# Gated-branch values: 512 weight columns per matmul and two k-chunks per load, instead of 256 columns and four k-chunks

## Chip, cores and metric

One Trainium2 core of a chip runs one launch. The metric is device time in microseconds (us); lower is better. Three timed runs of the kernel before gave 1669.36, 1669.82 and 1670.14 us, median 1669.82. All data are float32 in HBM.

## What is computed

One decoder layer over 512 prompt tokens and 64 sample tokens (8 sequences of 8), model width 1024: a SwiGLU feed-forward block, a mixing block, a second feed-forward block, each behind an RMS norm with conditioning. The change lies in the mixing block, in the value half of its gated branch:

```python
z = h @ w_in                      # w_in has 1024 rows; u, v, q, k, rv, rg, ga, gb are column ranges
v = layer_norm(gelu(v), gm_ln_g, gm_ln_b)      # v: 576 tokens x 1024 columns
o_a = gelu(u) * chunk_spatial_mix(v, ...)
o_b = head_rms(retention(rotary(q), rotary(k), rv, state)) * silu(rg)
```

The retention has 8 heads with 128 key and 256 value columns each.

## The kernel before

**Precision.** Large products are made in the float32r format of TensorE. A weight or activation is split into a high part (a cast on ScalarE, L180 in `split_w`, L188 in `split`) and a low remainder (a subtraction on VectorE, L181, L189). A product is the sum of three matmuls: high x high, low x high and high x low. The small products inside a retention head (L1376, L1438, L1454, L1467 to L1482) are plain float32, and the profile records each of these as two passes.

**Where the change sits.** The mixing block runs head by head. For head hd, `values_of` (matmuls L1346 and L1359) makes the head's values; `core(hd)` does the retention itself; `beside(hd)` gives the work that runs on TensorE next to that core. For heads 0 and 1 this work is `values` (matmuls L1576): columns 0 to 511 of v beside head 0 and 512 to 1023 beside head 1. Later heads have output products (`out_b`, L478) or the gates u beside them.

**`values` before.** The 512 columns of a head are done as two halves z of 256 columns. Each half has two loads of 512 KB (`load_w`: four k-chunks of 128 rows by 256 columns, DMA at L169, cast L180, subtraction L181). For each of five token tiles (four of 128 prompt tokens, and the 64 sample tokens, whose high and low parts fill one tile of 128) a PSUM bank is taken, and all 8 k-chunks are accumulated in it: 24 matmuls of 256 columns for a prompt tile, 16 for the sample tile. Then ScalarE takes the gelu out of PSUM at once (L1585; for the sample tile L1587, VectorE L1588 and L1589), and in the second half VectorE makes the statistics (L1591). A head has 224 such matmuls, the two heads 448.

**How the core is mixed in.** `core` is a generator. `tick(us)` (L225) subtracts a written cost from its delay and, when that is used up, issues its next piece. The pieces come at 0.5, 4.5, 8.5, 10.5, 12.5, 14.5, 18.5 and 20.5 us of ticked time. Before, `values` ticks after each token tile: 2.616 us for a prompt tile, 1.744 for the sample tile, 24.4 us in a head. The pieces, by number: 1, scores and transposes (L1376 to L1414), which need the rotated k from GpSimd (L1324); 2, four state products in four banks (L1438), evacuated by VectorE (L1441, L1443); 3, L1454; 4 and 5, the outputs (L1467 to L1482), two banks each; 6, squares and split; 7, two banks of sums over the squares (L1500), which VectorE reads only in piece 8 (L1522), and then four products, each in a bank of its own (L1511), evacuated by VectorE (L1515); 8, the scaling.

**Buffers and order.** PSUM has 8 banks in one pool (`bank`, bufs=8) for everything. Weight loads land in 3 raw buffers, split weights in 4. Banks and buffers are handed out, and the order of instructions on each engine is fixed, when the program is built: a planner goes by the order in which the code issues the work, but it puts an instruction that it takes to be ready ahead of an earlier one that it takes to be waiting. At run time each engine keeps that order.

Of the kernel before, what the change touches and what calls it, by code (L numbers as in the profile page):

```python
# [10 lines left out]
AF = mybir.ActivationFunctionType  # L11
ALU = mybir.AluOpType
# [3 lines left out]
P = 128  # L16
D = 1024
KC = D // P
# [3 lines left out]
NS = NB * LS  # L22
# [59 lines left out]
def layer_kernel(ctx: ExitStack, tc: tile.TileContext, a):  # L82
    nc = tc.nc
    PE, DVE, ACT, POOL = nc.tensor, nc.vector, nc.scalar, nc.gpsimd
# [22 lines left out]
    def nm(s):  # L107
        count[0] += 1
        return f"{s}_{count[0]}"
# [13 lines left out]
    def slot(shape, dt=F32):  # L123

        turn[1] += 1
        if now["slu"] and turn[1] % (NSLOT + NSLOT2) < NSLOT2:
            return now["slu"].tile(shape, dt, tag="c", name=nm("c"), bufs=NSLOT2)
        return now["sl"].tile(shape, dt, tag="c", name=nm("c"), bufs=now["slots"])
# [12 lines left out]
    def bank():  # L141
        return pp.tile([P, 512], F32, tag="ps", name=nm("ps"), bufs=8)
# [24 lines left out]
    def load_raw(src, k0, kc, c0, cols):  # L167
        raw = raw4([kc, cols])
        nc.sync.dma_start(  # L169
            out=raw, in_=src[k0 * P:(k0 + kc) * P, c0:c0 + cols].rearrange("(k p) c -> p k c", p=P)  # L170
        )
        return raw
# [5 lines left out]
    def split_w(raw, eng=None):  # L178
        hi, lo = high_low(list(raw.shape[1:]))
        ACT.copy(out=hi, in_=raw)  # L180
        now["lo"] = (eng or DVE).tensor_tensor(out=lo, in0=raw, in1=hi.bitcast(F32), op=ALU.subtract)  # L181
        return hi, lo

    def load_w(src, k0, kc, c0, cols, eng=None):
        return split_w(load_raw(src, k0, kc, c0, cols), eng)
# [39 lines left out]
    def tick(us):  # L225
        for s in list(side):
            s[1] -= us
            while s in side and s[1] <= 0:
                try:
                    s[1] += next(s[0])  # L230
                except StopIteration:
                    side.remove(s)
# [50 lines left out]
    for i in range(2):  # L283
        for n in range(NT):
            rows = P if n < 4 else NS
            t = first.tile([rows, 512], F32, name=nm("xt"))
# [185 lines left out]
    def proj(w, X, h, kc=KC, c0=0, ks=None, ps=None):  # L472
        ps = bank() if ps is None else ps
        wh, wl = w
        for k in ks or range(kc):
            xh, xl = X[k]
            for z, (s, m) in enumerate(((wh, xh), (wh, xl), (wl, xh))):
                PE.matmul(  # L478
                    ps[:, :H], lhsT=s[:, k, c0:c0 + P], rhs=m[:, HALF[h]],
                    start=k == 0 and z == 0, stop=k == kc - 1 and z == 2,  # L480
                )
        return ps
# [543 lines left out]
    for i in range(2):  # L1026
        for n in range(NT):
            m = P if n < 4 else NS
            ACT.activation(
                out=junk[0:m, i], in_=xtok[n, i], func=AF.Square, accum_out=ss[0:m, i, n:n + 1]  # L1030
# [54 lines left out]
    for c in range(KC):  # L1085
# [5 lines left out]
        out=t5, in0=r5, scalar=-0.5 / D, in1=r5, op0=ALU.mult, op1=ALU.mult)  # L1091
    steps["r51"] = lambda: DVE.scalar_tensor_tensor(
        out=t5, in0=s5, scalar=D * EPS, in1=t5, op0=ALU.add, op1=ALU.mult)
# [3 lines left out]
        out=xall[:, :, NP:T], in_=psS[:, 0:KC * NS].rearrange("p (c t) -> p c t", c=KC))  # L1097
# [22 lines left out]
    win = a["w_in"][0]  # L1120
    U0, V0, Q0, K0, RV0, RG0, GA0, GB0 = 0, 1024, 2048, 3072, 4096, 6144, 8192, 9216
# [158 lines left out]
    rts, tks = [], {}  # L1280
# [251 lines left out]
    def weights_b(hds, j):  # L1532
        kc = 2 * len(hds)
        return load_w(a["w_b"][0], 2 * hds[0], kc, j * (8 // kc) * P, 8 // kc * P)

    def out_b(hds, j, wb, cs=None):

        kc = 2 * len(hds)
        n = 8 // kc
        OB = [x for hd in hds for x in OBs[hd]]  # L1540
        for c in cs or range(n):
            t = slot([P, T])
            for h in range(2):
                ps = proj(wb, OB, h, kc=kc, c0=c * P)
                ACT.copy(out=t[:, HALF[h]], in_=ps[:, :H])
                tick(cost(kc))
            dst = accd[:, n * j + c, :]
            if hds[0] == 0:
                POOL.dma_start(out=dst, in_=t)
            else:  # L1550
                POOL.dma_start(out=dst, in_=t, accum_op=ALU.add)


    v = {}
# [3 lines left out]
    I32 = mybir.dt.int32  # L1558

    def weights_v(i, z):  # L1560
        return [load_w(win, 4 * kk, 4, V0 + i * 512 + z * 256, 256) for kk in range(2)]

    def values(i, z, ws):

        cl = slice(z * 256, (z + 1) * 256)
        for n in range(NT):
            ps = bank()
            for kx in range(KC):
                w = ws[kx // 4]
                if n < 4:  # L1570
                    xh, xl = (x[:, n * P:(n + 1) * P] for x in X[kx])
                    terms = ((xh, w[0]), (xl, w[0]), (xh, w[1]))
                else:
                    terms = ((tks["hs"][:, kx, :], w[0]), (tks["hs"][:, kx, :], w[1]))
                for y, (s, m) in enumerate(terms):
                    PE.matmul(  # L1576
                        ps[:, :256], lhsT=s, rhs=m[:, kx % 4, :], start=kx == 0 and y == 0,
                        stop=kx == KC - 1 and y == len(terms) - 1,
                    )
            m = P if n < 4 else NS  # L1580
            if z == 0:
                v[n, i] = slot([m, 512])
            t = v[n, i][:, cl]
            if n < 4:
                ACT.activation(out=t, in_=ps[:, :256], func=AF.Gelu_apprx_tanh)  # L1585
            else:
                ACT.copy(out=t, in_=ps[NS:P, :256])  # L1587
                DVE.tensor_tensor(out=t, in0=ps[0:NS, :256], in1=t, op=ALU.add)  # L1588
                ACT.activation(out=t, in_=t, func=AF.Gelu_apprx_tanh)  # L1589
            if z:  # L1590
                DVE.bn_stats(out=tks["stats"][0:m, n, i, :], in_=v[n, i])  # L1591
            tick((24 if n < 4 else 16) * 0.109)

    gains = []

# [52 lines left out]
    def weights_u(g):  # L1648
        return load_w(win, 0, KC, U0 + g * P, P)

    def gate_u(g, wu):
        t = slot([P, T])
        for h in range(2):
            ps = proj(wu, X, h)
            ACT.activation(out=t[:, HALF[h]], in_=ps[:, :H], func=AF.Gelu_apprx_tanh)
            tick(cost(KC))
        POOL.dma_start(out=ud[:, g], in_=t)
# [27 lines left out]
    def beside(hd):  # L1685

        if hd < 2:
            for z in range(2):
                yield lambda z=z: weights_v(hd, z), lambda w, z=z: values(hd, z, w)
        elif hd % 2 == 0:  # L1690
            for j in range(4):
                hds = hd - 2, hd - 1
                yield lambda j=j: weights_b(hds, j), lambda w, j=j: out_b(hds, j, w)
        elif hd < HEADS - 1:
            for g in range(2 * hd - 6, 2 * hd - 2):
                yield lambda g=g: weights_u(g), lambda w, g=g: gate_u(g, w)

    for hd in range(HEADS):
        wv = [load_w(win, 4 * i, 4, RV0 + hd * DV, DV) for i in range(2)]
        if hd:  # L1700
            states(hd)
        rv, rvs = values_of(hd, wv, rows[hd][:2])
        OBs.append([])
        q, k, *gates = rows.pop(hd)
        prev = core(hd, q, k, gates, rv, rvs, OBs[hd])
        start(prev, 0.5)
        if hd == 2:
            start(layer_norm(), 4.0)
        work = list(beside(hd))
        ready = None  # L1710
        for i, (weights, f) in enumerate(work):
            f(ready or weights())
            ready = None
            if i == 0 and hd + 1 < HEADS:
                rows[hd + 1] = fetch(hd + 1)
                if hd == 1:
                    fetch_gains()
                if hd == HEADS - 2:
                    fetch_mixers()
            if i == len(work) - 2 and i:  # L1720
                ready = work[i + 1][0]()
        if hd + 1 < HEADS:
            finish(prev)
        if hd == HEADS - 2:
            masks(0)
            masks(1)

    VT = [xx.tile([P, 4, T], F32, tag="x", name=nm("v"), bufs=4) for _ in range(4)]
    for i in range(2):
        for n in range(NT):  # L1730
            m, z = P if n < 4 else NS, NT * i + n
# [89 lines left out]
    for pr in ([0], [1], [2], [3], [4], [5], [6, 7]):  # L1821
# [4 lines left out]
        for h in range(2):  # L1826
            for c in pr:
                ps = proj(W[c], OA, h)
                t = sa[c][:, HALF[h]]
# [218 lines left out]
```

## Time and profile before

| what | value |
|---|---|
| median of the timed runs | 1669.82 us |
| span of the profiled execution, first to last instruction | 1665.5 us |
| median minus that span | 4.3 us |
| TensorE matmul busy | 1636.4 us |
| VectorE, ScalarE, GpSimd busy | 1154.7, 783.7, 287.8 us |
| `values` beside head 0 (with the core's pieces) | 755.62 to 794.16 us |
| `values` beside head 1 | 807.31 to 845.39 us |

The profiled execution gives its span; no other time of its own is recorded, so the 4.3 us around it are taken as they stand to the median. In the rows of the profile PE is TensorE's matmuls, PEld its weight loads, DVE is VectorE, ACT ScalarE, POOL GpSimd and SP the engine that issues loads. A row of the timeline has the start (us from the span's start), the duration, the engine, the line, the operation, output<-input, the shape (stationary rows x columns, then partitions x moving columns), and the count of merged instructions; in brackets stands the idle time of the engine before it and what ended it. Matmuls overlap in the pipeline, so the cost of a run of them is read from its start to the start of the next row, not from its duration.

### The profile page before, as it was taken

To read this page: it belongs to the slowest core of one execution; us is meant where nothing else is said; L and a number is where in the kernel's file an instruction comes from. 1 tells how busy PE (TensorE), PEld (TensorE's weight loads), DVE (VectorE), ACT (ScalarE), POOL (GpSimd) and SP (SyncE) were. 2 spreads that over 40 slices of the span, in tenths; PEclk is the share of its full clock that TensorE was granted. 3 is DMA by queue.
4 is the path that set the end of the run, shared out by engine and by line. 5 is a ranking of instruction groups with operands and counts; after the bars stand their busy time and mean duration, and the time that the engine had idled before them with its cause. 6 is when DMAs were issued, how large, how long until landed. Compare 5 with 4: busy or idle time off the path is not lost. (4 is left out here: it accounts for less than half of the span.)

```text
span 1665.5 us, 31366 instructions
## 1 busy us (share of the span) xinstructions
PE 1636.4 (98%) x12548; PEld 1574.8 (95%) x12548; DVE 1154.7 (69%) x1835; ACT 783.7 (47%) x1331; POOL 287.8 (17%) x372
## 2 busy tenths in 40 slices
PE   7999999999999999999999999999999999999997
PEld 4899999999999999999999999998999999999997
DVE  6867857576797777755688554677748868576773
ACT  5634524344564566544445454443236535243453
POOL 0000000000411110013346343454231000000002
PEclk9999999999999999999999999999999999999999
DMA  9553444332547676764457474799540333332321
GB/s 301 146 156 102 140 136 130 115 102 87 181 127 219 206 223 198 219 202 153 146 180 251 162 179 151 210 263 267 164 140 14 86 92 99 92 90 85 97 86 58
DMA packets 300212, 252.09 MB, mean 151 GB/s; under 512 B 13593, under 2 KB 260633, under 8 KB 300066
## 3 DMA queue, kind: packets, MB, share of 16 engines
q1 hardware_dynamic: 284594, 206.76, 41.2%
q0 software_dynamic: 13168, 40.97, 8.9%
q10 hardware_dynamic: 2304, 2.36, 0.4%
q8 instruction: 98, 1.61, 0.4%
q14 instruction: 48, 0.39, 0.1%
HBM read 207.01 MB, written 43.02 MB: 150 GB/s over the span
## 5 line engine op out<-in xcount | busy, mean ns | idle before, releaser
L644 PE MATMUL ps<-xa,whl 128*128 128x288 f32 x3000 | 421.0, 295 | 4.4 <-ACT whl L662 1.4
L644 PEld LDWEIGHTS ps<-xa,whl 128*128 128x128 f32 x3000 | 402.0, 189 | 17.3 <-issue 4.2
L644 PE MATMUL ps<-xs,whl 128*128 128x288 f32 x2040 | 289.4, 295 | 0.8 <-ACT sn L653 0.4
L644 PEld LDWEIGHTS ps<-xs,whl 128*128 128x128 f32 x2040 | 274.7, 189 | 10.9 <-issue 5.0
L672 DVE TENSOR_TENSOR whl<-wraw,whl 128x1024 fp32r<-128x1024 f32 x192 | 235.0, 1226 | 55.6 <-ACT whl L662 46.0
L662 ACT CAST whl<-wraw 128x1024 fp32r<-128x1024 f32 x192 | 200.3, 1048 | 109.5 <-DVE wraw L786 67.1
L478 PE MATMUL ps<-c,wd 128*128 128x288 f32 x1824 | 246.1, 295 | 0.0
L478 PEld LDWEIGHTS ps<-c,wd 128*128 128x128 f32 x1824 | 242.4, 189 | 3.7 <-issue 3.4
L478 PE MATMUL ps<-c,whl 128*128 128x288 f32 x1368 | 190.5, 297 | 1.1 <-ACT c L188 0.6
L478 PEld LDWEIGHTS ps<-c,whl 128*128 128x128 f32 x1368 | 182.8, 189 | 3.1 <-ACT c L188 1.1
L465 POOL TENSOR_TENSOR x<-x,s 128x64 f32<-128x64 f32 x72 | 34.6, 481 | 808.2 <-DVE s L464 781.0
L459 DVE SCALAR_TENSOR_TENSOR x<-ps,gate,x 128x288 f32<-128x288 f32 (+1 forms) x128 | 61.2, 481 | 117.1 <-PE ps L478 117.0
L181 DVE TENSOR_TENSOR whl<-wraw,whl 128x1024 fp32r<-128x1024 f32 x56 | 78.0, 1394 | 70.2 <-ACT whl L180 69.4
L653 ACT COPY sn<-ps 128x288 f32<-128x288 f32 x195 | 77.1, 398 | 104.2 <-PE ps L644 103.8
L945 ACT CAST wd<-wraw 128x640 fp32r<-128x640 f32 (+2 forms) x58 | 45.4, 783 | 105.6 <-PE ps L478 97.9
L1346 PE MATMUL ps<-whl,xx 128*128 128x256 f32 x768 | 91.5, 280 | 0.0
L1346 PEld LDWEIGHTS ps<-whl,xx 128*128 128x128 f32 x768 | 90.8, 188 | 0.0
L644 PE MATMUL ps<-xs,whs 128*128 128x288 f32 x480 | 69.8, 294 | 0.0
L180 ACT CAST whl<-wraw 128x1024 fp32r<-128x1024 f32 x56 | 58.5, 1049 | 22.7 <-PE ps L478 14.3
L644 PEld LDWEIGHTS ps<-xs,whs 128*128 128x128 f32 x480 | 65.6, 189 | 0.0
L662 ACT CAST whs<-wraw 128x512 fp32r<-128x512 f32 x62 | 38.4, 620 | 57.0 <-PE ps L644 46.7
L950 DVE TENSOR_TENSOR wd<-wraw,wd 128x640 fp32r<-128x640 f32 (+2 forms) x58 | 53.9, 929 | 9.8 <-ACT wd L945 9.8
(285 smaller groups left out, 2222.2 us busy)
## 6 DMA issues: line engine op xcount, KB each, us to landing
ada<-in_w_ada_dram SPq DMA_DIRECT2D x56, 512.0 KB
wraw<-in_w_in_dram SPq DMA_DIRECT2D x96, 256.0 KB
wraw<-in_w_gate_dram SPq DMA_DIRECT2D x88, 256.0 KB
wraw<-in_w_up_dram SPq DMA_DIRECT2D x88, 256.0 KB
wraw<-in_w_in_dram SPq DMA_DIRECT2D x32, 512.0 KB
wraw<-in_w_down_dram SPq DMA_DIRECT2D x32, 384.0 KB
wraw<-in_w_down_dram SPq DMA_DIRECT2D x32, 320.0 KB
accd<-c POOLq DMA_DIRECT2D x32, 288.0 KB, 6.0
```

Source lines behind the costliest of these rows:

```text
L180: ACT.copy(out=hi, in_=raw)
L181: now["lo"] = (eng or DVE).tensor_tensor(out=lo, in0=raw, in1=hi.bitcast(F32), op=ALU.subtract)
L459: DVE.scalar_tensor_tensor(out=x[:, o:o + w], in0=ps[:, :w], scalar=g[:, c, 0:1], in1=x[:, o:o + w], op0=ALU.mult, op1=ALU.add)
L465: return lambda: POOL.tensor_tensor(out=x[:, NP:T], in0=x[:, NP:T], in1=u, op=ALU.add)
L478: PE.matmul(ps[:, :H], lhsT=s[:, k, c0:c0 + P], rhs=m[:, HALF[h]], start=k == 0 and z == 0, stop=k == kc - 1 and z == 2,)
L644: PE.matmul(ps[:, :H], lhsT=s[:, j * P:(j + 1) * P], rhs=m[:, j, :], start=fresh and j == 0 and z == 0, stop=j == 3 and z == 2, skip_group ...
L653: ACT.copy(out=t, in_=ps[:, :H])
L662: ACT.copy(out=hl[:, 0], in_=src)
L672: now["lo"] = DVE.tensor_tensor(out=hl[:, 1], in0=src, in1=hl[:, 0].bitcast(F32), op=ALU.subtract)
L945: ACT.copy(out=hl[:, 0], in_=self.raw[c])
L950: DVE.tensor_tensor(out=lo, in0=self.raw[c], in1=hi.bitcast(F32), op=ALU.subtract)
L1346: PE.matmul(ps[:, :DV], lhsT=s, rhs=m, start=i == 0, stop=i == 23)
```

## The change

The two loads per half become four loads per head, of two k-chunks by 512 columns each; they are still 512 KB each and split by the same number of instructions. The loop over loads is now outermost: for each load, each of the five token tiles gets 6 matmuls of 512 columns (4 for the sample tile), into a bank that is taken at the first load and held until the last. Gelu, the sample tile's sum and the statistics come after the last load, on 512 columns at a time. Ticks come after each tile of each load: 1.32 us (0.88 for the sample tile), 24.64 us in a head. A head has 112 matmuls of 512 columns.

```diff
     def weights_v(i, z):
-        return [load_w(win, 4 * kk, 4, V0 + i * 512 + z * 256, 256) for kk in range(2)]
-
-    def values(i, z, ws):
-
-        cl = slice(z * 256, (z + 1) * 256)
+        return load_w(win, 2 * z, 2, V0 + i * 512, 512)
+
+    vps = {}
+
+    def values(i, z, w):
+
         for n in range(NT):
-            ps = bank()
-            for kx in range(KC):
-                w = ws[kx // 4]
+            if z == 0:
+                vps[n] = bank()
+            ps = vps[n]
+            for kk in range(2):
+                kx = 2 * z + kk
...
                     PE.matmul(
-                        ps[:, :256], lhsT=s, rhs=m[:, kx % 4, :], start=kx == 0 and y == 0,
-                        stop=kx == KC - 1 and y == len(terms) - 1,
+                        ps, lhsT=s, rhs=m[:, kk, :], start=kx == 0 and y == 0,
+                        stop=kx == KC - 1 and y == len(terms) - 1, skip_group_check=True,
                     )
-            m = P if n < 4 else NS
-            if z == 0:
-                v[n, i] = slot([m, 512])
-            t = v[n, i][:, cl]
-            if n < 4:
-                ACT.activation(out=t, in_=ps[:, :256], func=AF.Gelu_apprx_tanh)
-            else:
-                ACT.copy(out=t, in_=ps[NS:P, :256])
-                DVE.tensor_tensor(out=t, in0=ps[0:NS, :256], in1=t, op=ALU.add)
-                ACT.activation(out=t, in_=t, func=AF.Gelu_apprx_tanh)
-            if z:
-                DVE.bn_stats(out=tks["stats"][0:m, n, i, :], in_=v[n, i])
-            tick((24 if n < 4 else 16) * 0.109)
+            if z == 3:
+                m = P if n < 4 else NS
+                t = v[n, i] = slot([m, 512])
+                if n < 4:
+                    ACT.activation(out=t, in_=ps, func=AF.Gelu_apprx_tanh)
+                else:
+                    ACT.copy(out=t, in_=ps[NS:P])
+                    DVE.tensor_tensor(out=t, in0=ps[0:NS], in1=t, op=ALU.add)
+                    ACT.activation(out=t, in_=t, func=AF.Gelu_apprx_tanh)
+                DVE.bn_stats(out=tks["stats"][0:m, n, i, :], in_=t)
+            tick((6 if n < 4 else 4) * 0.22)
...
         if hd < 2:
-            for z in range(2):
+            for z in range(4):
                 yield lambda z=z: weights_v(hd, z), lambda w, z=z: values(hd, z, w)
```

## The prediction, made before the result was known

> **What bounds the kernel now.** I read the page first, then the timeline of the stage that the change touches, then who waited for whom there. The page:
>
> ```profile
> span 1665.5 us, 31366 instructions
> PE 1636.4 (98%) x12548; PEld 1574.8 (95%) x12548; DVE 1154.7 (69%) x1835; ACT 783.7 (47%) x1331; POOL 287.8 (17%) x372
> PE   7999999999999999999999999999999999999997
> PEclk9999999999999999999999999999999999999999
> ```
>
> TensorE's matmuls fill 98% of the span, so a saving must come out of matmul time, and an idle gap that the change puts between matmuls is paid in full. The stage is 742 to 845 us. Its two halves beside heads 0 and 1:
>
> ```profile
> 742.71 11.19 PE L1346 MATMUL ps<-whl,xx 128*128 128x256 f32 x94
> 753.74 2.05 PE L1359 MATMUL ps<-whl,hs 128*128 128x256 f32 x16
> 755.62 2.99 PE L1576 MATMUL ps<-whl,xx 128*128 128x256 f32 x24
> 759.52 1.16 PE L1376 MATMUL ps<-c,c 128*128 128x128 f32 x8 [0.91 <-POOL c L1324]
> ...
> 782.26 5.88 PE L1576 MATMUL ps<-whl,xx 128*128 128x256 f32 x48
> 787.97 0.69 PE L1500 MATMUL ps<-c,onesr 128*128 128x288 f32 x4
> 788.50 1.11 PE L1511 MATMUL ps<-c,c 128*128 128x256 f32 x8
> 789.45 2.98 PE L1576 MATMUL ps<-whl,xx 128*128 128x256 f32 x24
> ...
> 807.31 2.99 PE L1576 MATMUL ps<-whl,xx 128*128 128x256 f32 x24
> 810.14 1.05 PE L1376 MATMUL ps<-c,c 128*128 128x128 f32 x8
> ...
> 838.48 0.44 PE L1500 MATMUL ps<-c,onesr 128*128 128x288 f32 x2
> 838.77 0.39 PE L1511 MATMUL ps<-c,c 128*128 128x256 f32 x2
> 839.60 0.54 PE L1500 MATMUL ps<-c,onesr 128*128 128x288 f32 x2 [0.44 <-DVE c L189]
> 839.97 0.88 PE L1511 MATMUL ps<-c,c 128*128 128x256 f32 x6
> ```
>
> The value matmuls (L1576) and the core's pieces follow each other without a gap, except 0.91 us before L1376 in head 0 (the rotated k was late from GpSimd) and 0.44 before L1500 in head 1. The waits and the use of the engines in the stage:
>
> ```profile
> ACT c L1585 <- PE ps L1576: 26.6, 14, 4.2
> 755.60:794.10 38.50, 37.59 (x330) 36.27 (x329) 21.23 (x31) 18.82 (x33) 13.74 (x15) 1.00 0.39 126
> 807.30:845.40 38.10, 37.66 (x331) 36.34 (x330) 20.94 (x30) 17.42 (x32) 12.42 (x13) 1.00 0.45 146
> ```
>
> The first row says that ScalarE's gelu waits for TensorE, 26.6 us in 14 waits, and not the other way round. The other two are the windows, with the columns PE, PEld, DVE, ACT, POOL, granted clock, DMA share and GB/s: the clock is full, DMA and the other engines have room. So only three things can move the time: the cost of a 512-column matmul, the place of the core's pieces among them, and the banks.
>
> **The change, part by part.** *Matmuls removed and added.* 94 matmuls of 256 columns take 753.74 - 742.71 = 11.03 us, 117.3 ns each; the 448 of `values` go at 448 x 117.3 = 52.6 us. In their place come 224 of 512 columns. No row shows a float32r matmul of that width. The nearest are 288 columns, and a plain-float32 pass of 256 columns:
>
> ```profile
> 525.42 3.31 PE L644 MATMUL ps<-xa,whl 128*128 128x288 f32 x24
> 528.57 3.32 PE L644 MATMUL ps<-xs,whl 128*128 128x288 f32 x24
> 764.38 1.02 PE L1438 MATMUL ps<-c,c 128*128 128x256 f32 x4
> 765.25 0.81 PE L1438 MATMUL ps<-c,c 128*128 128x256 f32 x3
> ```
>
> 288 columns: 3.15 us for 24, 131.25 ns. Upper end: 512 columns cost twice 256, 234.6 ns, and nothing is saved; the cost per column is nearly the same in both rows (0.458 and 0.456 ns), which speaks for it. A line through the two widths (13.95 ns for 32 columns, 0.436 each) gives 117.3 + 256 x 0.436 = 228.9. Lower end: the fifth plain pass starts 0.87 us after the first (the second answer begins with it), 217 ns; a pass that holds the array nearly twice as long as 256 float32r columns do shows only 0.424 ns per column of 512, so part of today's 117.3 may be a fixed cost of a matmul. I take 226, nearer to the line, because its rows are float32r with weight and activation operands: 224 x 226 = 50.6, a saving of 1.9 us; the ends give 4.0 (217) and 0.
>
> The Trainium skill has a rule for this, "TensorE: Matmul & The Clock Gate", section "Back-to-back issue gap": N/2.4 + 2.5 ns when warm, so 109 ns at 256 and 216 at 512 columns. The trace does not agree at 256 (117.3); for a long pass it does (217). By the rule's 512 the saving would be 52.6 - 48.4 = 4.2 us.
>
> *Core pieces.* Six of the eight pieces hold matmuls, before and after, so the number of breaks in the run of value matmuls stays, unless the planner splits more. Piece 1 moves: it came after the first token tile, 24 matmuls; now it comes after the first 6, 6 x 226 = 1.36 us. Head 0's k cannot be there sooner:
>
> ```profile
> 756.01 1.30 DVE L181 TENSOR_TENSOR whl<-wraw,whl 128x1024 fp32r<-128x1024 f32 x1 [1.47 <-ACT whl L180]
> 757.24 0.75 DVE L1323 TENSOR_TENSOR c<-c,rope 128x576 f32<-128x576 f32 x1
> 758.06 1.40 POOL L1324 TENSOR_TENSOR c<-c,c 128x576 f32<-128x576 f32 x1 [1.83 <-DVE c L1323]
> 806.54 1.44 POOL L1324 TENSOR_TENSOR c<-c,c 128x576 f32<-128x576 f32 x1 [0.69 <-DVE c L1323]
> ```
>
> It ends at 759.46, behind a weight split on VectorE that the change leaves there. If L1376 stands right behind the first 6 matmuls, TensorE waits from 756.98 to 759.46, 2.5 us instead of 0.91: +1.6, and behind it on TensorE queue value matmuls that are ready. If the planner sees the wait, it puts the next tile's matmuls first, as it put L1511 between the two L1500 at 838.48: then the wait may shrink below 0.91, at best -0.9. I take +0.5. In head 1 k is there at 807.98, before 807.31 + 1.36 = 808.67: 0; the cover is 0.7 us.
>
> *Banks.* After the first load's tiles five of the eight banks are held, until the last load; three are left for the core. Pieces 3 to 5 take one or two at a time, and ScalarE empties them between. Piece 2 takes four when four are held; the fifth tile's bank then waits for VectorE's first evacuation, and VectorE can be behind by a split (1.30 us above): between 0 and 1.3 a head, mostly covered by the other tiles' matmuls, +0.2 over both. Piece 7 is the tight one. It now comes after the first tile of the last load: two banks for L1500, held until piece 8, and four products that want four more, with one bank free and a second when the first gelu is out. The products are evacuated by
>
> ```profile
> 789.20 2.46 DVE L1515 SCALAR_TENSOR_TENSOR S<-S,ps 128x512 f32<-128x512 f32 x4
> L1511 PE MATMUL ps<-c,c 128*128 128x256 f32 x64 | 9.2, 281 | 0.0
> L1585 ACT ACTIVATE c<-ps 128x256 f32<-128x256 f32 x16 | 6.1, 384 | 26.6 <-PE ps L1576 26.6
> L1487 ACT COPY c<-ps 128x512 f32<-128x512 f32 x16 | 9.4, 587 | 12.9 <-PE ps L1482 12.6
> ```
>
> 0.62 us each. Matmuls of the next tiles (1.36 us a tile, banks already theirs) can stand between the products, so I take 0.3 per head, 0.6 in all; below nothing is excluded, since no wait stands there now. The price without that cover is the second rival.
>
> *The rest, at nothing.* Eight loads stay eight, with the same bytes, casts and splits. On SP three of four loads are now issued after the tiles of the load before, behind the fetch for the next head; with a DMA share of 0.39 and 6.3 us of matmuls per load, a load stays early, and without that cover it would cost its delay. Gelu falls from 16 of 0.384 us to 8 of about 0.6 (the 512-wide L1487 copy takes 0.587) but all at the end of a head, where the next head's first bank is needed one at a time, every 2.8 us (24 matmuls of 117.3): ScalarE's 5 evacuations of about 0.6 us are hidden by that.
>
> **Sum** on the span of 1665.5: -1.9 + 0.5 + 0.2 + 0.6 = -0.6, so 1664.9; with the 4.3 us between span and median, **1669.2 us**. A measurement of this kernel can tell about 0.2%, 3.3 us, from no change: this is none.
>
> **The rivals.**
>
> *The wide matmul is cheap.* If a 512-column matmul costs 217 ns and the fillers hide the waits (k down by 0.4, no bank wait), the sum is -4.0 - 0.4 = -4.4: 1665.4 us, faster. For it: the plain pass at 217. Against it: 0.458 and 0.456 ns per column at 256 and 288, no sign of a fixed part there. Both conditions must hold to pass 3.3 us. The page's rule above stands with this rival.
>
> *Three banks choke piece 7.* If the planner leaves the four products in a row, each waits until VectorE has emptied the one before: latency 0.28 us (the 281 ns of an L1511), 0.24 for its two matmuls (8 in 0.95 us), 0.62 evacuation, 1.14 us. Four take 3 x 1.14 + 0.24 = 3.7 us in place of 0.95: +2.7 a head, +5.4 for two. With k's +1.6 and the saving of 1.9 this gives +5.1: 1674.9 us, slower. It decides when fewer than two spare banks are there at piece 7 and nothing stands between the products. For it: 5 + 2 banks held. Against it: the fill at 838.48 to 839.97, and a gelu that frees a bank within about 1 us.
>
> *Nothing in it.* The width is neutral (234.6 ns) and the small waits come as above: +1.3, 1671.1 us, within 0.2%.
>
> **How the numbers follow.** Forecast 0.47, cheap wide matmul 0.25, choked banks 0.16, nothing in it 0.12. Faster by over 0.2%: 0.25; within 0.2%: 0.59; slower: 0.16. The range runs from 1665.0, just under the cheap case, to 1673.0, which takes in the neutral case with k's full 1.6 us and one bank wait and leaves out most of the choked case. The likeliest case's own range is 1666.5 to 1671.
>
> **What would show it.** In the profile after: value matmuls 128x512, x224; a burst of them read start to start, at 226 ns (217: first rival; 235: third). Between 755 and 795: the idle time before L1376 in head 0, expected 0 to 2.5 us, and whether value matmuls of a second tile stand ahead of it. Before the L1511 rows: no idle time over 0.5 us, and value matmuls between them; a wait for DVE L1515 before each is the second rival. The stage from the first value matmul to the next head's L1346 should go from 38.5 and 38.1 us to about 38 and 37.5. The forecast would be wrong by a wait of several us that I did not place, such as a bank of the next head's L1346 held by a late gelu, or a late weight split of the second load.

## The result and the profile after

The changed kernel takes 1671.14 us (median of 21 runs, 1669.18 to 1674.01) where the kernel before takes 1669.69 on the same chips (21 runs, 1667.57 to 1671.10): a ratio of 1.0012, with a 95% interval of 1.0007 to 1.0018. It is slower by 1.2 to 3.0 us, inside the 0.2% that the prediction called no change; the forecast of a small gain was not met. The profiled execution took 1672.98 us for a span of 1671.2, so 1.8 us lie around the span (the prediction took 4.3, because it compared a quick execution's span with a median).

The page of the changed kernel, its first lines:

```profile
span 1671.2 us, 30923 instructions
PE 1639.1 (98%) x12324; PEld 1567.1 (94%) x12324; DVE 1156.2 (69%) x1833; ACT 782.5 (47%) x1319; POOL 288.2 (17%) x372
```

224 matmuls fewer, as the change says. The share of TensorE's busy time over the whole span tells nothing here; the stage does. The windows run from the first matmul beside a head to the next head's first L1346, beside heads 0, 1 and 2 (columns: length, busy time of PE, PEld, DVE, ACT, POOL, granted clock, DMA share, GB/s). First the changed kernel:

```profile
758.40:796.35 37.95, 37.41 (x219) 30.50 (x218) 20.95 (x28) 16.57 (x25) 13.73 (x15) 1.00 0.44 141
809.50:848.46 38.96, 37.64 (x219) 30.56 (x218) 20.41 (x31) 15.24 (x24) 14.11 (x13) 1.00 0.48 154
861.60:899.90 38.30, 36.90 (x298) 35.22 (x297) 36.36 (x64) 18.16 (x35) 26.50 (x33) 1.00 0.72 237
sum 115.21, PE 111.95 PEld 96.28 DVE 77.73 ACT 49.98 POOL 54.35; mean PE 37.32 PEld 32.09 DVE 25.91 ACT 16.66 POOL 18.12
```

Then the third stretch and the sum of the kernel before (its first two stand in the prediction):

```profile
858.55:895.50 36.95, 36.71 (x298) 35.27 (x297) 34.07 (x58) 18.05 (x35) 26.80 (x32) 1.00 0.71 225
sum 113.55, PE 111.97 PEld 107.89 DVE 76.24 ACT 54.29 POOL 52.96; mean PE 37.32 PEld 35.96 DVE 25.41 ACT 18.10 POOL 17.65
```

This is the result in two rows. TensorE's busy time is the same, 111.95 and 111.97 us, though 224 wide matmuls replaced 448 narrow ones. The stretches are 1.66 us longer, 115.21 against 113.55, and all of that is idle time: 3.26 us after, 1.58 before. Head 0 gains 0.55 us, head 1 loses 0.86, and head 2, whose matmuls the change does not touch, loses 1.35. From head 3 on, the stretches are equal in both kernels (36.51 and 36.46 us, alternating).

Where the idle time lies, by the waits of TensorE between 735 and 900 us in the changed kernel (engine, line, releaser: total, times, longest):

```profile
PE ps L1376 <- POOL c L1324: 3.0, 3, 1.3
PE ps L1414 <- POOL h L1409: 0.3, 1, 0.3
```

The same of the kernel before, and the row of its wait beside head 2 (that of head 0 stands in the prediction):

```profile
PE ps L1376 <- POOL c L1324: 1.1, 2, 0.9
PE ps L1500 <- DVE c L189: 0.4, 1, 0.4
```

```profile
860.54 1.16 PE L1376 MATMUL ps<-c,c 128*128 128x128 f32 x8 [0.24 <-POOL c L1324]
```

And in the timeline of the changed kernel, beside heads 0, 1 and 2:

```profile
758.39 3.39 PE L1579 MATMUL ps<-whl,xx 128*128 128x512 f32 x14
762.32 1.16 PE L1376 MATMUL ps<-c,c 128*128 128x128 f32 x8 [0.54 <-POOL c L1324]
...
789.76 0.70 PE L1500 MATMUL ps<-c,onesr 128*128 128x288 f32 x4
790.29 0.40 PE L1511 MATMUL ps<-c,c 128*128 128x256 f32 x2
790.53 1.33 PE L1579 MATMUL ps<-whl,xx 128*128 128x512 f32 x5
...
793.56 2.02 PE L1579 MATMUL ps<-whl,xx 128*128 128x512 f32 x8
795.42 1.09 PE L1579 MATMUL ps<-whl,hs 128*128 128x512 f32 x4
796.35 0.87 PE L1346 MATMUL ps<-whl,xx 128*128 128x256 f32 x6
...
809.49 1.56 PE L1579 MATMUL ps<-whl,xx 128*128 128x512 f32 x6
812.37 1.16 PE L1376 MATMUL ps<-c,c 128*128 128x128 f32 x8 [1.32 <-POOL c L1324]
...
861.58 1.76 PE L478 MATMUL ps<-c,whl 128*128 128x288 f32 x12
864.47 1.16 PE L1376 MATMUL ps<-c,c 128*128 128x128 f32 x8 [1.13 <-POOL c L1324]
866.74 0.44 PE L1414 MATMUL ps<-ident,h 128*128 128x128 f32 x2 [0.27 <-POOL h L1409]
```

Three things are to be read here. *The width:* the eight matmuls at 793.56 are followed at 795.42, 232.5 ns each; four at 795.42 by 796.35, the same. That is 0.454 ns per column, as at 256 (0.458). *The banks:* pieces 7 and 8 lie at 789.76 to 793.56, value matmuls stand between the L1511, and no row shows a wait. *k:* the L1376 waits for GpSimd's L1324 in all three heads, and in head 1, where there was no wait before, for 1.32 us.

### The profile page after: what moved, and what is told of

The parts are those of the page before. It is cut to its first block, busy times and chain, and to the rows that moved or that the text cites. A ratio compares the mean times of both kernels' runs of the same rounds, so it can differ in the third digit from the quotient of the medians.

```text
span 1671.2 us, 30923 instructions
## 1 busy us (share of the span) xinstructions
PE 1639.1 (98%) x12324; PEld 1567.1 (94%) x12324; DVE 1156.2 (69%) x1833; ACT 782.5 (47%) x1319; POOL 288.2 (17%) x372
## 5 line engine op out<-in xcount | busy, mean ns | idle before, releaser
L644 PE MATMUL ps<-xa,whl 128*128 128x288 f32 x3000 | 425.4, 297 | 4.4 <-ACT whl L662 1.4
L644 PEld LDWEIGHTS ps<-xa,whl 128*128 128x128 f32 x3000 | 406.4, 191 | 17.3 <-issue 4.2
L1346 PE MATMUL ps<-whl,xx 128*128 128x256 f32 x768 | 91.5, 279 | 0.0
L1346 PEld LDWEIGHTS ps<-whl,xx 128*128 128x128 f32 x768 | 90.9, 188 | 0.2
```

Of the source, the lines that this page charges most:

```text
L644: PE.matmul(ps[:, :H], lhsT=s[:, j * P:(j + 1) * P], rhs=m[:, j, :], start=fresh and j == 0 and z == 0, stop=j == 3 and z == 2, skip_group ...
L1346: PE.matmul(ps[:, :DV], lhsT=s, rhs=m, start=i == 0, stop=i == 23)
```

## Why k is late: VectorE at the turn of the heads

VectorE and GpSimd of the changed kernel, from the end of head 0 to k of head 1 (the next value matmul stands at 809.49):

```profile
801.61 1.28 DVE L1592 BATCH_NORM_STATS2 stats<-c 128x6 f32<-128x512 f32 x2
802.81 0.67 DVE L1590 TENSOR_TENSOR c<-ps,c 64x512 f32<-64x512 f32 x1
803.50 0.76 DVE L1320 TENSOR_TENSOR c<-c,rope 64x576 f32<-64x576 f32 x1
...
805.06 0.69 DVE L1592 BATCH_NORM_STATS2 stats<-c 64x6 f32<-64x512 f32 x1
...
806.49 1.99 POOL L1324 TENSOR_TENSOR c<-c,c 128x576 f32<-128x576 f32 x1 [11.02 <-DVE c L1323]
807.20 1.89 DVE L1322 TENSOR_TENSOR c<-c,rope 64x576 f32<-64x576 f32 x1
809.13 0.76 DVE L1323 TENSOR_TENSOR c<-c,rope 128x576 f32<-128x576 f32 x1
809.83 1.22 DVE L181 TENSOR_TENSOR whl<-wraw,whl 128x1024 fp32r<-128x1024 f32 x1
809.97 2.34 POOL L1324 TENSOR_TENSOR c<-c,c 128x576 f32<-128x576 f32 x1 [0.70 <-DVE c L1323]
```

And VectorE of the kernel before (the next value matmul at 807.31; its L1324, 1.44 us at 806.54, stands in the prediction):

```profile
798.83 0.68 DVE L1591 BATCH_NORM_STATS2 stats<-c 64x6 f32<-64x512 f32 x1
799.52 0.75 DVE L1320 TENSOR_TENSOR c<-c,rope 64x576 f32<-64x576 f32 x1
800.29 0.75 DVE L1322 TENSOR_TENSOR c<-c,rope 64x576 f32<-64x576 f32 x1
801.08 1.23 DVE L181 TENSOR_TENSOR whl<-wraw,whl 128x1024 fp32r<-128x1024 f32 x1
```

In the kernel before, gelu and statistics of a tile came every 24 matmuls; one statistic was left at the turn. Now all five tiles of a head end in its last load, so three statistics and the last tile's addition (L1590) queue on VectorE in front of and among the next head's rotary. The rotary of q and k begins 5.99 us ahead of the value matmuls (803.50 against 809.49) in place of 7.79 (799.52 against 807.31): 1.80 later. A split of 1.23 that stood in it is now a statistic of 0.69: 0.54 sooner. GpSimd's last step, now beside a split on VectorE, takes 2.34 in place of 1.44: 0.90 later. Together 2.16; k is there 2.83 us after the first value matmul (809.97 + 2.34 - 809.49 = 2.82), where it was at 0.67 (806.54 + 1.44 - 807.31).

A late k alone would not have cost this in head 1. Before, L1376 stood behind 24 matmuls, 2.83 us; now it stands behind 6 wide ones, 1.4 us.

At the turn from head 1 to head 2 the changed kernel has the same three statistics and the addition, and besides them two steps of the layer norm over v (L1637) in front of the rotary, which in the kernel before come behind its start:

```profile
848.83 0.75 DVE L1637 SCALAR_TENSOR_TENSOR c<-c,mv,c 128x512 f32<-128x512 f32 x1
...
852.63 0.75 DVE L1637 SCALAR_TENSOR_TENSOR c<-c,mv,c 128x512 f32<-128x512 f32 x1
```

## The experiments

What follows is measured by the three stretches of the profiled execution, beside heads 0, 1 and 2, because they came again within 0.05 us in the one repeat made, while the times of one kernel scatter by 3.4 to 7.1 us from run to run (more on this in the last section). The table has them, counted from start to start of the matmuls in the trace. Each ratio is to runs of the kernel before taken beside that kernel, whose own median was between 1669.69 and 1670.17 us:

| kernel | head 0 | head 1 | head 2 | sum | median us (runs) | ratio to before, 95% |
|---|---|---|---|---|---|---|
| before | 38.53 | 38.08 | 36.96 | 113.57 | 1669.69 (21) | |
| after | 37.96 | 38.97 | 38.32 | 115.25 | 1671.14 (21) | 1.0012, 1.0007 to 1.0018 |
| after_again | 37.96 | 39.02 | 38.31 | 115.29 | 1670.93 (1) | |
| e1_halves | 38.59 | 37.47 | 37.80 | 113.86 | 1672.10 (11) | 1.0014, 1.0005 to 1.0023 |
| e2_late_core | 37.96 | 37.84 | 39.92 | 115.72 | 1673.94 (6) | 1.0030, 1.0018 to 1.0041 |
| e3_stats_later | 37.93 | 38.98 | 36.70 | 113.61 | 1670.89 (12) | 1.0007, 0.9997 to 1.0016 |
| e5_stats_behind | 38.12 | 37.38 | 37.29 | 112.79 | 1668.32 (11) | 0.9994, 0.9985 to 1.0003 |
| e6_splits_behind | 38.45 | 37.38 | 37.27 | 113.10 | 1668.76 (12) | 0.9994, 0.9986 to 1.0003 |
| b3_splits_stats_behind | 37.97 | 38.06 | 37.26 | 113.29 | 1668.71 (12) | 0.9993, 0.9983 to 1.0002 |
| b1_early_core | 38.46 | 37.96 | 37.57 | 113.99 | 1668.89 (11) | 1.0000, 0.9991 to 1.0009 |
| b4_early_core_late_k | 38.49 | 37.97 | 37.54 | 114.00 | 1671.63 (1) | |
| b5_late_k | 38.59 | 38.07 | 36.96 | 113.62 | 1670.47 (1) | |
| b6_early_core_later_k | 38.85 | 40.12 | 37.58 | 116.55 | 1671.65 (1) | |
| b7_later_k | 38.58 | 38.27 | 36.97 | 113.82 | 1670.34 (1) | |

Theory: the width is neutral, and the loss is k, late behind the statistics, met by a piece that now stands early. Rivals: the held banks, or the wide matmul itself.

**after_again**, the changed kernel once more, unaltered.

> The changed kernel once more, unaltered, to see how well the stretches repeat. Theory: 37.96, 38.97 and 38.32 us within 0.1 each, while the span as a whole moves by 1 to 4 us with the short drops of the granted clock outside the stretches.

The stretches repeat within 0.05 us, and the waits are the same (L1376 3.0 us in three, L1414 0.3), while the time is 2.05 us below that of the first profiled execution. So the 1.7 us of the stretches belong to the kernel, and 2 us outside them can come or go from one execution to the next.

**e1_halves**: the changed loads, banks and order, each product in two matmuls of 256.

```diff
-                    PE.matmul(
-                        ps, lhsT=s, rhs=m[:, kk, :], start=kx == 0 and y == 0,
...
+                    for cl in (slice(0, 256), slice(256, 512)):
+                        PE.matmul(
+                            ps[:, cl], lhsT=s, rhs=m[:, kk, cl], start=kx == 0 and y == 0 and cl.start == 0,
```

> The changed kernel, but each 512-column matmul is issued as two of 256 columns into the two halves of the held bank; loads, ticks, held banks and the late gelu stay. I read the three stretches from the first matmul beside head 0, 1 and 2 to the next head's L1346 (before 38.53, 38.08, 36.96, sum 113.57; changed 37.96, 38.97, 38.32, sum 115.25). My theory, that width is neutral (233 against 2 x 117.3 ns) and the loss is k coming late to L1376 in heads 1 and 2: sum within 0.5 us of 115.25. Rival, that wide matmuls are themselves the loss: sum back to about 113.6. The prediction's step of 1.9 us saved by width: sum up to about 117.

The halves cost about 116 ns each. Taking each value matmul up to the next matmul's start and leaving out the waits, the value matmuls of both heads sum to 54.4 us before, 54.2 after and 54.1 here: the width is neutral. The expected sum of 115.25 was missed all the same; 113.86 is nearly the number that the rival named. Taken by itself the sum would speak for wide matmuls as the loss, but the cost of the matmuls does not, and the run does not separate width from order: with twice the instructions the planner made another order at the turn. The same three statistics stood there, but the rotary of q and k began 6.58 us ahead of head 1's matmuls in place of 5.99, and L1324 ran beside no split (1.42 in place of 2.34). So k came at 1.31 us and the wait of head 1 was gone (37.47), while L1376 waited in heads 0 and 2, 2.0 us in all. Its median lies higher than its stretches say; why stays open.

**e2_late_core**: the core's first piece 1.3 us later in the plan.

```diff
-        start(prev, 0.5)
+        start(prev, 1.8 if hd < 2 else 0.5)
```

> The changed kernel with the core of heads 0 and 1 started 1.3 us of ticked time later (delay 1.8 in place of 0.5), so that piece 1 follows two token tiles. k in head 1 came 2.82 us after the first value matmul; two tiles take 2.8 us. Theory (late k): the wait of 1.32 us in head 1 falls to 0.2 or less, that stretch from 38.97 to about 37.8; head 2 is not touched, 38.3; sum about 114.0. Rival (only the early place of piece 1 costs, not VectorE's late work): the same in head 1, and the wait in head 2 unexplained. Rival (held banks): no change in the sum.

Head 1 gains 1.13 us, with L1376 now behind 12 wide matmuls and a wait of 0.22. But the shift also pushed the core's own last steps further into the next turn: L1522 on VectorE came 12.60 us ahead of head 2's matmuls in place of 14.28, three layer-norm steps (L1637) stood in front of head 2's rotary in place of two, and the rotary began 4.07 us ahead of the matmuls in place of 5.72. The row of this kernel beside head 2:

```profile
865.24 1.16 PE L1376 MATMUL ps<-c,c 128*128 128x128 f32 x8 [3.21 <-POOL c L1324]
```

The wait moved from one head to the next and grew, so the expected sum of 114.0 was missed (115.72). A shift of the core by itself is no remedy.

**e3_stats_later**: the statistics are owed and issued later, head 0's beside head 1's second load, head 1's at the start of the layer norm.

```diff
-                DVE.bn_stats(out=tks["stats"][0:m, n, i, :], in_=t)
+                owed.append((m, n, i))
+            if i and z == 1:
+                pay()
...
+        while owed:
+            pay()
+            yield 0.7
```

> The changed kernel with the ten statistics (0.69 us each on VectorE) taken away from the turn of the heads: those of head 0 beside the second load of head 1, those of head 1 at the start of the layer norm beside head 2. Theory (VectorE's work at the turn makes k late): k in head 1 ready about 1 to 2 us earlier, wait 1.32 down to 0.4 or less; in head 2 the wait of 1.13 and the 0.27 before L1414 shrink too, unless the statistics collide there with the layer norm; sum about 113.5 to 114.3. Rival (early place of piece 1 alone): waits as they are, sum 115.2.

The sum came as expected (113.61), but not for the expected reason, and in head 1 nothing changed (38.98, k at 2.83): the planner, which puts a step whose data are there ahead of one that it takes to be waiting, had put the postponed statistics back at the turn. In head 2 k came at 1.48 us in place of 2.84, the wait fell under 0.1, and the stretch from 38.32 to 36.70. Yet at that turn, too, three statistics still stand in front of and among the rotary (now at another line); two of them are in this row, the third begins at 855.31:

```profile
851.87 1.27 DVE L1567 BATCH_NORM_STATS2 stats<-c 128x6 f32<-128x512 f32 x2
```

What left the turn is the layer norm, which the edit holds back until the last statistic is issued. Without the two L1637 the rotary begins 6.55 us ahead of head 2's matmuls in place of 5.72, and L1324, which in the changed kernel begins 0.04 us behind a layer-norm step on VectorE, begins 0.03 ahead of one here and takes 1.43 us in place of 1.96; 0.83 and 0.53 make the 1.36 by which k is sooner. So in head 2 the layer norm's steps are part of the loss. Of the statistics the run shows that a later place in the program did not make them later on their engine.

**e5_stats_behind**: the same, with an order written out: each statistic behind the last rotary step issued by then.

```diff
-        DVE.tensor_tensor(out=x, in0=x, in1=rope[:, 0], op=ALU.mult)
+        now["rot"] = DVE.tensor_tensor(out=x, in0=x, in1=rope[:, 0], op=ALU.mult)
...
+        in_order([now["rot"], DVE.bn_stats(out=tks["stats"][0:m, n, i, :], in_=v[n, i])])
...
+            if i and z == 0:
+                pay()
```

> The changed kernel with the ten statistics written behind the rotary of the next head on VectorE (head 0's behind the rotary of head 1, head 1's behind that of head 2), so that three or more of them, 0.65 to 0.69 us each, leave the queue in front of the k that L1376 waits for. Theory (VectorE's late evacuation work delays k): k in head 1 ready at about +0.3 to +1.4 us after the first value matmul in place of +2.83, the wait of 1.32 us gone or under 0.2, stretch 1 about 37.7; in head 2 k at +1 to +1.6 in place of +2.84, stretch 2 about 37.0; stretch 0 unchanged at 37.96; sum 112.5 to 113.2, that is 2 to 2.7 us below the changed kernel's 115.25 and just below 113.57 of before. Rival (held banks or the wide matmuls cost the time): sum stays at 115.

VectorE (behind k's last rotary step there), GpSimd and TensorE of this kernel at the same turn:

```profile
804.43 3.05 DVE L1567 BATCH_NORM_STATS2 stats<-c 128x6 f32<-128x512 f32 x5
```

```profile
804.59 1.44 POOL L1324 TENSOR_TENSOR c<-c,c 128x576 f32<-128x576 f32 x1 [0.69 <-DVE c L1323]
```

```profile
807.08 1.56 PE L1583 MATMUL ps<-whl,xx 128*128 128x512 f32 x6
808.47 1.05 PE L1376 MATMUL ps<-c,c 128*128 128x128 f32 x8
```

All five statistics now stand behind the rotary; k is there at 806.03, a microsecond ahead of the first value matmul, and L1376 follows six wide matmuls without a wait. Heads 1 and 2 give back 1.59 and 1.03 us, and the sum is 2.46 below the changed kernel's, with the same matmuls, banks and loads. That settles it: the loss was the order on VectorE. In head 1 that is the order of the statistics; in head 2 this edit holds back the layer norm as e3 does, and the runs don't part the two there. Against the kernel before, the stretches are 0.78 us shorter; by the median this can't be told from no change.

**e6_splits_behind** adds an order for the splits of the third and fourth load, and **b3_splits_stats_behind** gives the kernel before both orders.

```diff
+        if z > 1:
+            in_order([now["rot"], now["lo"]])
```

> As e5_stats_behind, and the weight splits of the third and fourth load of each head are written behind that head's own rotary on VectorE. In head 0 the split that stands before the last rotary step waits 1.47 us for ScalarE, and k comes at +3.8 us in every kernel so far. Theory: k of head 0 moves to about +1.8 us, the 0.54 us wait there goes; stretch 0 about 37.3 to 37.5, the others as in e5; sum about 112.2. Rival (k in head 0 hangs on the late rope table or GpSimd): stretch 0 unchanged.

> The kernel before with the same two orders: statistics behind the next head's rotary, and the splits of the second half's loads behind the head's own rotary. If the width is neutral and only k's lateness matters, it should end where e6 ends: waits of 0.91 in head 0 and 0.24 in head 2 gone, stretches about 37.6, 37.7, 36.7, sum about 112.0. If the wide matmuls save something of their own, e6 is lower by it (prediction: 1.9); if the held banks cost, e6 is higher.

In e6 head 0's k comes at 2.53 in place of 3.94, but 0.35 us of the wait stays at L1376, a wait of 0.46 at L1414 follows and the stretch is 38.45, not the expected 37.3 to 37.5: nothing is won. In b3 no wait is left at L1376, but waits of 0.39 to 0.45 stand at L1414 and L1500, and the sum is 113.29. Both sums are about 1 us above those expected (112.2 and 112.0), with the same idle time in both, 1.27 and 1.26 us. With the same orders the wide kernel with held banks (113.10) and the narrow one (113.29) differ by 0.19 us: that is the worth of width, banks and the place of the core's pieces together, once the order on VectorE is the same. A variant of the kernel before that only holds banks wasn't tried.

**b1_early_core**: the kernel before, with the core's pieces allowed after half a tile.

```diff
+                if kx == 3:
+                    tick((12 if n < 4 else 8) * 0.109)
...
-            tick((24 if n < 4 else 16) * 0.109)
+            tick((12 if n < 4 else 8) * 0.109)
```

> The kernel before with ticks twice as fine (after 12 matmuls of 256 columns), so that the core's pieces come as early as in the changed kernel (1.4 us after the first value matmul) while gelu and statistics stay spread. Rival (early place alone is the loss): waits before L1376 of about 1.3 us in head 1, first two stretches up by 1 to 2 us from 76.6. Theory (late VectorE): k in head 1 is there 0.67 us after the first value matmul, so no wait in head 1; in head 0 the wait of 0.91 grows to at most 2.4 or is filled; head 2 stays at 36.96; sum 113.0 to 115.1 by head 0 alone.

L1376 of head 1 moved from 2.83 to 1.41 us behind the first value matmul; k was there even sooner (0.50 us ahead of it), and the stretch is 37.96. Beside head 1 the earlier piece alone costs nothing. Head 2, expected to stay at 36.96, came out at 37.57: k was there 2.54 us after the first matmul in place of 1.95, with a layer-norm step (L1638, at 854.93) in front of its rotary, and L1376 waited 0.84 us in place of 0.24. So the finer ticks have a price of their own in head 2, and it again goes by way of VectorE.

**b4_early_core_late_k** and **b5_late_k** were to make k late by extra statistics in front of head 1's rotary, whose output is written over later: four on b1 and two on the kernel before.

```diff
+                if hd == 1 and n == 3:
+                    extra = [now["rot"]] + [
+                        DVE.bn_stats(out=tks["stats"][:, j, 1, :], in_=tks["rope"][:, 0, 0:512]) for j in range(4)
+                    ]
```

> b1_early_core (256-column matmuls, nothing held, core pieces as early as in the changed kernel) with four extra statistics of 0.65 to 0.69 us put on VectorE in front of head 1's k rotary, 2.7 us in all. In b1 k was there 0.50 us before the first value matmul of head 1, and piece 1 came 1.41 us after it, without a wait. Theory (the loss needs both an early piece 1 and a k that VectorE delays): k at about +2.2 us, or +3 if GpSimd runs beside a weight split; a wait of 0.8 to 1.6 us before L1376 in head 1, stretch 1 from 37.96 to 38.8 to 39.6, like the 38.97 of the changed kernel. Rival (wide matmuls or held banks): no wait, 38.0.

> The kernel before with two extra statistics in front of head 1's k rotary, 1.3 to 1.4 us. Theory: k moves from +0.66 to about +2.0 us in head 1, but piece 1 comes at +2.83 there, behind a whole token tile, so no wait: stretch 1 within 0.2 of 38.08. If lateness of VectorE costs by itself, the stretch grows by about 1.3 us.

Neither tells anything: k moved only to 0.72 and 0.89 us, ahead of L1376 in both. In b4 four statistics took 2.47 us, but L1322 no longer ran beside GpSimd and fell from 1.89 to 0.75, so k moved by 1.22. The expected wait of b4 did not come, and b5's delay was too small to test anything.

**b6_early_core_later_k** and **b7_later_k** are the same with seven and four.

> The loads of before, the first core piece after 12 matmuls of 256, and seven extra statistics on VectorE in front of the rotary of head 1's k (they do nothing else; what they write is written over later). Four extra ones moved k by 1.22 us, to 0.72 us after the first value matmul, and TensorE came to L1376 at 1.41 without a wait. Theory (in head 1 the loss needs both the earlier piece and the later k): three more at about 0.6 us bring k to 2.0 to 2.7, TensorE waits 0.6 to 1.3 us before L1376 in head 1, and the stretch beside head 1 is 38.6 to 39.3 us instead of 37.96. Rival (TensorE finds other work, or the loss of the changed kernel in head 1 is its wide matmuls or its banks): no wait, 38.0.

> Before, with four extra statistics in front of the rotary of head 1's k and nothing else: the first core piece stays behind 24 matmuls, at 2.83 us. Theory (both are needed): k comes at 1.5 to 2.3 us, later than the 1.41 us at which the early piece stands and sooner than 2.83; no wait before L1376 in head 1, the stretch stays at 38.1. Rival (a late k alone costs time, whatever stands ahead of the piece): a wait of over 0.3 us there, the stretch 38.5 or more.

TensorE and GpSimd of b6 (early piece, late k):

```profile
809.07 1.57 PE L1581 MATMUL ps<-whl,xx 128*128 128x256 f32 x12
812.50 1.16 PE L1381 MATMUL ps<-c,c 128*128 128x128 f32 x8 [1.86 <-POOL c L1324]
```

```profile
810.14 2.31 POOL L1324 TENSOR_TENSOR c<-c,c 128x576 f32<-128x576 f32 x1 [4.65 <-DVE c L1323]
```

And of b7 (late k alone):

```profile
808.74 2.99 PE L1581 MATMUL ps<-whl,xx 128*128 128x256 f32 x24
811.64 1.16 PE L1381 MATMUL ps<-c,c 128*128 128x128 f32 x8
```

```profile
809.18 2.41 POOL L1324 TENSOR_TENSOR c<-c,c 128x576 f32<-128x576 f32 x1 [2.88 <-DVE c L1323]
```

(L1381 is the L1376 of the others.) In b7 k is there 2.85 us after the first value matmul, later than the 1.5 to 2.3 expected, and within 0.02 of the changed kernel's 2.83; behind 24 matmuls it costs no wait, and the stretch is 38.27 against 38.08. In b6 the same kind of delay with the early piece costs 1.86 us of waiting, and the stretch grows from 37.96 to 40.12. k was later than expected there too (3.38), so wait and stretch passed the expected 1.3 and 39.3. In both, L1324 ran beside a split and took 2.3 to 2.4 us, not the 1.4 that I had reckoned with. In b7 k was there only 0.05 us before L1376 began, so that case lies at the edge of a wait. Beside head 1 the four cases b1, b7, b6 and before make the square: early piece alone, no loss; late k alone, no wait; both, the loss. And it arises with matmuls of 256 and no bank held. Head 0, which the edits do not aim at, grew by 0.39 us from b1 to b6 as well (its wait at L1376 from 0.88 to 1.25): another program gets another order elsewhere too, so differences of a few tenths between kernels are not to be read closely.

## Why the prediction was wrong, step by step

- **Matmuls: -1.9 predicted, -0.2 measured.** TensorE's busy time beside heads 0 and 1 went from 37.59 + 37.66 to 37.41 + 37.64. I took 226 ns, between 217 of a plain-float32 pass and 234.6 of twice the narrow one; it is 232.5. The equal cost per column at 256 and 288, which the prediction itself quoted, was the better guide, and the plain pass, another type, the wrong neighbour. By the formula for an isolated matmul in the Trainium skill, "TensorE: Matmul & The Clock Gate", section "Back-to-back issue gap", it would be 216; the trace disagrees at 512 (232.5) as it did at 256 (117.3).
- **Head 0's k: +0.5 predicted, -0.37 measured.** The planner put 14 wide matmuls ahead of L1376, not 6, and the wait fell from 0.91 to 0.54; the prediction had named this way of it and its limit, -0.9.
- **"In head 1 k is there at 807.98, before 807.31 + 1.36 = 808.67: 0; the cover is 0.7 us." This is the step that failed, measured at +1.32.** It moved the piece that waits and left in place the time of what it waits for. k is made on VectorE and GpSimd, and the change moves work on VectorE: k lost 2.16 us, three times the cover.
- **"The rest, at nothing": the same mistake from the other end.** The prediction saw that all gelus fall at the end of a head and asked only whether ScalarE can free the banks; it can. It did not follow what stands behind each gelu, a statistic on VectorE, in front of the next head's rotary. Head 2, which was in no term of the sum, pays at the same place: 0.9 more at L1376 (1.13, before 0.24) and 0.27 at L1414. There two steps of the layer norm came in front of the rotary as well; with these alone held back (e3) the wait was gone, and why the planner put them sooner than in the kernel before stays open.
- **Banks: +0.8 predicted, 0 measured**; no wait at L1511. The 0.44 before L1500 in head 1 is even gone.

The sum of the idle terms: -0.37 + 1.32 - 0.44 + 0.9 + 0.27 = 1.68, the 3.26 - 1.58 of the windows. With the busy time's -0.02 this is the 1.66 of the stretches; the ratio's 1.2 to 3.0 us holds it. Of the rivals, the cheap wide matmul and the choked banks are refuted. "Nothing in it" was right in the width, and its 1671.1 us meets the median by chance: its waits, head 0's k and the banks, are not those that came.

## What to carry to other kernels

When a change gathers the results of a stage at its end, list every step behind each result, on every engine, and ask what the next stage has queued there: here 0.6 us statistics stood in front of a rotary that TensorE waits for. A cover is the difference of two times, and both must be worked out anew; the piece moved up 1.4 us and what it waits for moved back 2.2. Under a planner that reorders, as here, a step that may be late is kept late by an order on its engine and not by its place in the program (e3 against e5).

## What else the runs showed of the hardware

**Two elementwise engines slow each other.** GpSimd's L1324 took 1.44 us beside statistics (e5, at 804.59) and 2.31 to 2.41 beside a split (after, b6, b7); VectorE's L1322 took 0.75 and, beside L1324, 1.89 (after, at 807.20). The rows look as if the two took turns: in the changed kernel the split ends at 811.05 and L1324 1.26 us later, a little under those 1.44; the L1324 of q ends at 808.48 and L1322, begun at 807.20, 0.61 us later, a little under its 0.75. So a step that is put off also changes the duration of its neighbours: this swallowed half of b4's delay. The Trainium skill, "GPSIMD Engine Reference", section "1. Specifications", says that GpSimd's interfaces to the memory are shared with VectorE and contended by VectorE instructions with two inputs there. The rows agree: the split, with two inputs, slows L1324, and the statistic, with one, does not.

**Short drops of the granted clock go with much of the scatter.** In some executions TensorE runs at half clock for 3.4 us (a mean of 0.57 over 4.00 us) at places whose code is the same in both kernels. The windows, the same columns as above, of the profiled execution of after:

```profile
51.00:55.00 4.00, 4.00 (x21) 4.00 (x20) 2.71 (x8) 2.97 (x4) 0.00 (x0) 0.57 0.69 218
451.00:454.20 3.20, 3.20 (x15) 3.20 (x15) 1.36 (x3) 3.10 (x6) 0.42 (x1) 0.50 0.26 92
```

and of before:

```profile
51.00:55.00 4.00, 4.00 (x32) 3.95 (x32) 2.92 (x8) 3.43 (x5) 0.00 (x0) 1.00 0.60 184
451.00:454.20 3.20, 3.20 (x25) 3.10 (x24) 2.33 (x4) 2.23 (x6) 0.00 (x0) 1.00 0.00 0
```

In the first of these windows 21 matmuls are done in place of 32, in the second 15 in place of 25. At the 131 ns of a 288-column matmul these 21 missing ones are 2.75 us, and the first value matmul comes 2.77 us later after than before (758.39 against 755.62): nearly half of the 5.7 us by which the spans of the two first profiles differ, and nothing of the change. Between its first 40 us and its last 12 the repeat of the changed kernel has one such drop (at 1306 us), this execution three (the third at 1307 us), the first profile of before none. Ahead of these drops stands a stretch in which TensorE has little to do. The one ahead of the first drop in after, and the same stretch in before:

```profile
47.60:51.00 3.40, 1.45 (x17) 0.54 (x9) 2.10 (x3) 2.43 (x5) 0.00 (x0) 1.00 1.08 293
```

```profile
47.60:51.00 3.40, 1.44 (x16) 0.95 (x9) 2.35 (x4) 2.21 (x5) 0.00 (x0) 1.00 1.12 307
```

But 1.45 us of work in 3.4 brought a drop in the one and 1.44 none in the other, so the gap alone does not decide it. The Trainium skill, "TensorE: Matmul & The Clock Gate", section "What's actually happening", has the clock judged in windows of 3413 ns that run on whatever the kernel does, and halved after an idle one. The trace agrees in the length of the drops and in the windows: the three drops of this execution begin at 51.42, 450.78 and 1307.53 us, 117 and 251 times 3.413 us apart. Counted on from its own drop at 28.54 us, the windows of before cut the gap in two (45.61 to 49.02 with 2.49 us of matmuls, 49.02 to 52.43 with 2.37), where after has 1.46 us in the one from 48.01 to 51.42. But TensorE was busy for 1.46 and 1.79 us in the windows ahead of the first two drops, so idle can't mean without work. Nor is the busy time all: 2.38 us in a window of e6 (from 1136.89) brought a drop, and 1.60 in one of after_again (from 46.17) none. Over 30 runs of the kernel before, mean times rise from 1667.3 us at a mean granted clock of 0.998 (5 runs) to 1670.9 at 0.995 (8 runs): as wide as nearly all the differences of this study, and the reason to read such a change from its stage. In the 21 runs of the changed kernel the tie is looser; at 0.996 alone they go from 1670.64 to 1673.91 us, so the drops are not the whole of the scatter.
